# Hybrid encoder layer on one core: latent bias summed in part on VectorE, and three smaller edits in the front

## The chip, the cores and the metric

The kernel runs on one core of a Trainium2 chip. The metric is the device time in microseconds (us) of one execution; the time of a kernel is the median of several runs.

## The reference, cut to what matters

One encoder layer over 1024 tokens with 1024 features, batch 1, all in float32. It normalises and modulates the input, projects it, runs a pooling branch and a latent-attention branch, and projects back:

```python
c_act = silu(c)
shift, scale, gate = split(c_act @ ada_w + ada_b, 3)
xn   = rmsnorm(x, norm_g) * (1 + scale) + shift
proj = xn @ w_in
u_pool, g_pool, q_lat, kv_lat, k_rope_raw, g_attn = split(proj)   # 512, 512, 256, 128, 32, 512 columns
y_pool = multiscale_pool(u_pool, pool_w, pool_scale) * silu(g_pool)
q  = rmsnorm(q_lat, g_q_lat) @ w_uq           # 8 heads of 64 + 32 (rope)
kv = rmsnorm(kv_lat, g_kv_lat) @ w_ukv        # 8 heads of 64 (key) + 64 (value)
k  = concat(k_nope, k_rope_raw for every head)
q, k = rmsnorm(q, g_qnorm), rmsnorm(k, g_knorm)  # over the 96 features of a head, then rope
y_attn = softmax(q k^T / sqrt(96)) v * silu(g_attn)
out = x + gate * (concat(y_pool, y_attn) @ w_out)
```

Three things matter here. `shift` goes through the projection as a bias: (x*r*a + shift) @ W = r * ((x*a) @ W) + shift @ W, so every block of projected columns needs a bias row `shift @ W`. The columns q_lat, kv_lat and k_rope_raw (416 together) are called the latent block. The norm of a key takes in the squares of the 32 rope columns, which all heads share.

## The kernel before, in words

Features stand on the 128 partitions in eight blocks (index `k`), tokens in eight tiles of 128 (index `t`). Float32 products are made from two parts, a high part of reduced precision and the rest, as three matmuls (high by high, high by low, low by high). Five queues run beside each other: TensorE (T), VectorE (V), ScalarE (A), GpSimd (G) and SyncE (SY), which issues the loads. Each runs its instructions in order.

**Front** (lines 207 to 474, under `tc.manual_schedule()`: the order is the program's; instructions of later parts may be put between by the framework's planner).

1. `cb` is silu(c), laid over all partitions; it is made in two blocks of 512 columns, each by TensorE into a PSUM bank and by ScalarE from there (L218, L219).
2. For each `k`: `lat_load` loads a block of the scale weights (`asc`), of x and of the latent weights `wlr[k]`; `lat_scale` multiplies `asc` by `cb` and sums over the columns (`mod_col`, L108, a VectorE product with a running sum) into one column of `a_raw`, makes `a_col` from it, and ScalarE makes the high part of the scaled x (`xh[k]`); `lat_low` makes the rest. TensorE accumulates the latent block of seven token tiles (`lat_mm`, L234), and of the eighth behind the loop.
3. The shift: eight more `mod_col` (`shift_col`) fill `sh_raw`, and two additions (L382, L403) make `shift` for `k` 0 to 3 and 4 to 7.
4. `lat_bias(k)` (L397) multiplies `shift[:, k]`, laid over 128 columns, by `wlr[k]` and accumulates all eight `k` in the bank `pbl`. Each is two matmul instructions in the trace. The first four `k` run ahead of the end of feature tile 0, the other four behind it and behind the first two blocks of tile 1.
5. Behind them, in the same bank but at column 448, TensorE makes the bias of feature tile 0 (L409, eight `k`, one column each, 16 matmul instructions). ScalarE copies `pbl` to `lbias` (L428), VectorE copies column 448 into `bias_fm` (L464).
6. The up-projection's weights are scaled and split (`wuqh`, `wuql`, `wkvh`, `wkvl`: L424 to L430).
7. `lat_end(t)` (L449 to L452) scales the latent tile by the token's norm, adds `lbias`, and ScalarE sums the squares of its q and kv columns. `lat_rms` (from L459 on) makes the latent norms of four token tiles at a time. `v_range` (L437 to L443) takes the maximum over `pv`, a TensorE sum of squares of the value weights.

Feature tiles are the other twelve blocks of 128 projected columns. `fm_mm(i, ...)` (L170) runs the blocks `k0` to `k1` of tile `i`, six matmuls each, into two banks; `fm_weights` loads and splits a tile's weights; `fm_fold` (L152, L154) multiplies a tile's weights by `shift` on GpSimd and adds up the eight blocks in three halvings, and `fm_bias` sums the result over the partitions on TensorE. Tiles 2, 4, 6 and 8 to 11 are folded.

PSUM: the pool `psB` has seven banks (`bk`), the pool `psC` one (`sbk`, tag `sm`). `pst`, `pbl`, `pv`, the transposes `pt` of the next part and the small sums `psb` share that one bank, each waiting until the last reader of the one before it is done.

**Up-projection and pooling** (lines 477 to 715, ordered by the planner). Per token tile, `up_tr` transposes the latent tile (`pt`, L532; ScalarE copies it to `lth`, VectorE makes `ltl`), `up_tok` makes queries, keys and values (L548, L558) and their sums of squares `ssq`; its last two lines square the 32 rope columns of the tile on ScalarE, with a running sum into `kr2` (L568). `gains_of_qk`, called at the second token, ends with eight small GpSimd products (L513, L514). After the loop come `rope_key` and `up_norm`, which adds `kr2` to the key's sums and takes the reciprocal root. Then feature tiles 2 to 10 run with the pooling, and the attention and the output projection follow, in an order written by hand again.

Of the kernel before, what the change touches and what calls it, by code (L numbers as in the profile page):

```python
# [17 lines left out]
P = 128  # L18
# [40 lines left out]
def body(ctx, tc, small, cond, xT, ada_sc, ada_sh, ada_gt, w_lat, w_fm, pool_w, w_uq, w_ukv, gains, pos, w_out, out):  # L59
# [46 lines left out]
    def mod_col(dst, w, cb):  # L106

        V.scalar_tensor_tensor(w, w, 1.0, cb, ALU.mult, ALU.mult, accum_out=dst)  # L108
# [27 lines left out]
    def sbk(name):  # L136
        return smallp.tile([P, 512], F32, tag="sm", name=name)
# [11 lines left out]
        return raw, hi, lo  # L149

    def fm_fold(pb):
        G.tensor_tensor(pb, pb, shift.unsqueeze(2).broadcast_to([P, NK, P]), ALU.mult)  # L152
        for n in (4, 2, 1):
            G.tensor_tensor(pb[:, :n], pb[:, :n], pb[:, n:2 * n], ALU.add)  # L154

# [52 lines left out]
    with ExitStack() as pa:  # L208
# [41 lines left out]

        def lat_scale(k):

            mod_col(a_raw[:, k:k + 1], ascs[k], cb)
            V.tensor_scalar(a_col[:, k:k + 1], a_raw[:, k:k + 1], ab1[:, k:k + 1], ng_s[:, k:k + 1],
                            ALU.add, ALU.mult)
            A.activation(wlh[k], wlr[k], AF.Copy)
            V.tensor_tensor(wll[k], wlr[k], f32(wlh[k]), ALU.subtract)
            for c_ in (slice(0, 512), slice(512, S)) if k == 0 else (slice(0, S),):
                A.activation(xh[k][:, c_], xrs[k][:, c_], AF.Copy, scale=a_col[:, k:k + 1])
# [134 lines left out]
        pbl = sbk("pbl")  # L394

        def lat_bias(k):
            T.matmul(pbl[:, :LAT], shift[:, k:k + 1].broadcast_to([P, P]), wlr[k], start=k == 0, stop=k == NK - 1)  # L397

        for k in range(4):
            lat_bias(k)  # L400
# [2 lines left out]
        V.tensor_tensor(shift[:, 4:], sh_raw[:, 4:], adab_s[:, 4:8], ALU.add)  # L403
        fm_mm(0, fhi0, flo0, 6, 8)
        fm_mm(1, fhi1, flo1, 0, 2)
        for k in range(4, NK):
            lat_bias(k)
        for k in range(NK):
            T.matmul(pbl[:, 448:449], fraw0[:, k, :], shift[:, k:k + 1], start=k == 0, stop=k == NK - 1,  # L409
                     skip_group_check=True)  # L410


        wuqh = mp.tile([P, 2, 768], F32R, tag="wuqh", name="wuqh")
# [47 lines left out]

        for t in range(2):
            lat_end(t)
        V.tensor_copy(bias_fm[:, 0:1], pbl[:, 448:449])  # L464
        fm_mm(1, fhi1, flo1, 2, 5)
        pv = sbk("pv")
        T.matmul(pv, ones, sqv, start=True, stop=True)
        fm_mm(1, fhi1, flo1, 5, 6)
        for t in range(2, NK):
            lat_end(t)  # L470
            if t == 6:
                lat_rms(0, 4)
        v_range()
        lat_rms(4, NK)
# [15 lines left out]
    def gains_of_qk():  # L490


        gm = QT[:, NK - 1].rearrange("p h d -> p (h d)")[:, 0:192].rearrange("p (i c) -> p i c", i=3)
        for i, g_ in enumerate((ggk, gqr, gkr)):
            n = g_.shape[1]
            V.scalar_tensor_tensor(gm[:, i, :n], g_, -1.0, g_, ALU.mult, ALU.max)
            V.tensor_reduce(p2[:, i:i + 1], gm[:, i, :n], AX.X, ALU.max)
        V.tensor_scalar(p2[:, 0:3], p2[:, 0:3], 1e-15, 1e15, ALU.max, ALU.min)
        V.tensor_scalar(p2[:, 0:3].bitcast(I32), p2[:, 0:3].bitcast(I32), 0x7F800000, None, ALU.bitwise_and)
        V.tensor_tensor(p2[:, 3:4], p2[:, 1:2], p2[:, 2:3], ALU.mult)  # L500
        V.tensor_tensor(p2[:, 3:4], p2[:, 3:4], p2[:, 0:1], ALU.max)
        V.tensor_scalar(esc, p2[:, 3:4], 1.0 / 1024.0, None, ALU.mult)
        V.tensor_scalar(nesc, p2[:, 3:4], -1.0 / 1024.0, None, ALU.mult)
        V.reciprocal(ksc, p2[:, 3:4])
        V.tensor_scalar(ksc, ksc, 8.0, None, ALU.mult)
        V.tensor_scalar(gkr, gkr, p2[:, 1:2], None, ALU.mult)
        V.reciprocal(p2[:, 1:2], p2[:, 1:2])
        V.tensor_scalar(gqr, gqr, p2[:, 1:2], None, ALU.mult)
        cs, sn = KA[:, :, 0:16], KB[:, :, 0:16]
        for ta, tb_, g in ((TA, TB, gqr), (KA, KB, gkr)):  # L510
            for c_ in (slice(16, 32), slice(0, 16)):
                gb = g[:, c_].unsqueeze(1).broadcast_to([P, NK, 16])
                G.tensor_tensor(ta[:, :, c_], cs, gb, ALU.mult)  # L513
                G.tensor_tensor(tb_[:, :, c_], sn, gb, ALU.mult)  # L514

    V.tensor_tensor(ggk, gn[:, 0, 0:64], gn[:, 1, 0:64], ALU.mult)

    def rope_key():
# [21 lines left out]
    def up_tok(t, lth, ltl):  # L540
# [14 lines left out]
        for n in range(2):  # L555
            pk = bk(f"pk{t}{n}")
            for i, (l, r) in enumerate(((lth, wkvh), (lth, wkvl), (ltl, wkvh))):
# [6 lines left out]
        A.activation(VT[:, t, :, 0:64], pkv[1], AF.Copy, scale=rkv[:, t:t + 1])  # L564
        V.scalar_tensor_tensor(VT[:, t, :, 65:129], pkv[1], rkv[:, t:t + 1], VT[:, t, :, 0:64],
                               ALU.mult, ALU.subtract)
        jk = upl.tile([P, 32], F32, tag="jk", name=f"jk{t}", bufs=2)
        A.activation(jk, lat[:, t, 384:416], AF.Square, accum_out=kr2[:, t:t + 1])  # L568

    def up_norm():  # L570
        V.tensor_tensor(ssq[:, 1], ssq[:, 1], kr2.unsqueeze(2).broadcast_to([P, NK, H]), ALU.add)
        tmp = upl.tile([P, 2, P], F32, tag="lth", name="rh", bufs=2)
        rsqrt_(tmp, rqk.rearrange("p a t h -> p (a t h)"), ssq.rearrange("p a t h -> p (a t h)"), 2 * NK * H, 96)
        V.tensor_scalar(rqk[:, 0], rqk[:, 0], 128.0 * HD ** -0.5, None, ALU.mult)
        V.tensor_scalar(rqk[:, 1], rqk[:, 1], ksc, None, ALU.mult)
# [4 lines left out]
    for t in range(NK):  # L580
# [5 lines left out]
        up_tok(t, *lt)  # L586
        lt = nxt
    A.activation(yp[0], yp[0], AF.Silu, bias=bias_fm[:, 0:1])
    rope_key()
    up_norm()  # L590
    up.close()


# [600 lines left out]
```

## Time and profile before

| | |
|---|---|
| median of 3 runs | 501.46 us (501.36 to 502.86) |
| profiled execution, own time | 500.05 us |
| its span | 498.3 us |
| TensorE matmuls busy | 464.9 us (93%) |
| VectorE busy | 355.9 us (71%) |
| ScalarE busy | 253.8 us (51%) |
| GpSimd busy | 234.4 us (47%) |
| granted TensorE clock, mean | 0.996 |

The rows below count from the span's start. PE is TensorE's matmuls, PEld its weight loads, DVE is VectorE, ACT ScalarE, POOL GpSimd, SPq the queue that issues loads. L12 is line 12 of the kernel; where a helper records an operation the line is the helper's. A busy share over the whole span mixes stages with different limits, so stretches are read one by one.

### The profile page before, as it was taken

How to read it: one execution, taken by the hardware profiler on the slowest of the kernel's cores; microseconds unless marked ns; L12 is line 12 of the kernel's file. 1: busy time of each engine (PE TensorE's matmuls, PEld its weight loads, DVE VectorE, ACT ScalarE, POOL GpSimd, SP SyncE). 2: the span in 40 equal slices, each digit the busy share in tenths (PEclk: the TensorE clock that was granted, in tenths of full speed). 3: DMA queues.
4: the chain of work that ended last, by engine and by line, in shares of the span. 5: the costliest groups of instructions: out<-in, count | busy, mean ns of one | idle time of the engine just before them, and what ended most of it. 6: DMA issues, size and time to landing. Idle time of an engine off the chain costs nothing.

```text
span 498.3 us, 7657 instructions
## 1 busy us (share of the span) xinstructions
PE 464.9 (93%) x2956; PEld 355.0 (71%) x2956; DVE 355.9 (71%) x565; ACT 253.8 (51%) x338; POOL 234.4 (47%) x190
## 2 busy tenths in 40 slices
PE   5999998999999999999989888898898969999997
PEld 3999876898888888785555555555555658888886
DVE  4888849999999853577677887877867985913221
ACT  3756038993203030226878888888899861001000
POOL 1950040201242949448869796787869780000000
PEclk9999999999999999999999999999999999999999
DMA  8894442000102110144786779779982836753333
GB/s 300 332 307 159 171 142 65 6 1 7 47 1 91 34 58 27 57 86 95 170 148 138 162 145 176 152 151 163 224 175 63 160 113 231 276 182 129 126 128 126
DMA packets 117046, 66.33 MB, mean 133 GB/s; under 512 B 105873, under 2 KB 107793, under 8 KB 117010
## 3 DMA queue, kind: packets, MB, share of 16 engines
q1 hardware_dynamic: 117010, 65.85, 49.9%
q8 instruction: 23, 0.38, 0.3%
q14 instruction: 13, 0.11, 0.1%
HBM read 35.43 MB, written 4.19 MB: 80 GB/s over the span
## 4 chain that ended last, share of the span: by engine, by line
PE 49%; DVE 22%; ACT 10%; POOL 10%; issue 5%; DMA 3%; SPq 0%; ACTq 0%; DVEq 0%; POOLq 0%
PE ops L974 14%; PE fps L170 8%; PE st L800 4%; PE pq L548 3%; ACT ph L824 3%; PE lps L234 3%; DVE bp L808 3%; POOL fraw L152 3%; ACT p L819 3%; DMA wlr<-in_w_lat 2%; PE rs L730 2%; PE av L849 2%; PE st L804 2%; POOL s L614 2%; DVE ph L831 2%
## 5 line engine op out<-in xcount | busy, mean ns | idle before, releaser
L831 POOL TENSOR_TENSOR ph<-p,ph 128x1024 f16<-128x1024 f32 x49 | 105.9, 2168 | 13.1 <-ACT ph L824 10.2
L170 PE MATMUL fps<-xh,whi 128*128 128x512 f32 x192 | 62.0, 404 | 0.5 <-ACT whi L147 0.5
L170 PE MATMUL fps<-xh,wlo 128*128 128x512 f32 x192 | 59.3, 390 | 0.1
L170 PE MATMUL fps<-xl,whi 128*128 128x512 f32 x192 | 59.3, 390 | 0.0
L800 PE MATMUL st<-q,k 97*128 97x512 f16 x192 | 49.5, 379 | 6.7 <-ACT p L819 6.6
L804 PE MATMUL st<-k,q 97*128 97x512 f16 x192 | 48.2, 379 | 8.0 <-ACT p L819 6.4
L824 ACT ACTIVATE ph<-p 128x1024 f16<-128x1024 f32 x49 | 51.7, 1055 | 0.5
L152 POOL TENSOR_TENSOR fraw<-fraw,shift 128x1024 f32<-128x1024 f32 x7 | 22.7, 3237 | 60.8 <-DVE wlo L148 53.8
L808 DVE TENSOR_REDUCE bp<-st 128x1 f32<-128x1024 f32 x32 | 39.0, 1220 | 5.2 <-PE st L804 3.4
L170 PEld LDWEIGHTS fps<-xh,whi 128*128 128x128 f32 x192 | 35.5, 189 | 9.0 <-ACT whi L147 1.0
L170 PEld LDWEIGHTS fps<-xh,wlo 128*128 128x128 f32 x192 | 36.0, 188 | 8.1 <-DVE wlo L148 0.5
L170 PEld LDWEIGHTS fps<-xl,whi 128*128 128x128 f32 x192 | 36.1, 188 | 7.7
L935 ACT ACTIVATE owhi<-oraw 128x1024 fp32r<-128x1024 f32 (+1 forms) x10 | 8.8, 885 | 54.0 <-DMA oraw<-in_w_out 54.0
L819 ACT ACTIVATE p<-st,bp,esc 128x1024 f32<-128x1024 f32 x25 | 30.1, 1204 | 9.4 <-DVE bp L809 9.0
L804 PEld LDWEIGHTS <-q 97*128 97x128 f16 x192 | 16.6, 97 | 25.6 <-issue 10.9
L800 PEld LDWEIGHTS <-k 97*128 97x128 f16 x192 | 16.6, 97 | 21.5 <-issue 8.3
L624 ACT ACTIVATE dh<-s 128x1024 fp32r<-128x1024 f32 x4 | 4.2, 1062 | 51.9 <-DVE s L621 51.9
L819 ACT ACTIVATE p<-st,ebias,esc 128x1024 f32<-128x1024 f32 x24 | 28.9, 1203 | 2.5 <-PE st L800 1.3
L850 PE MATMUL av<-VT,ph 128*128 128x65 f16 x256 | 26.4, 193 | 2.9 <-POOL ph L831 2.9
L849 PE MATMUL av<-VT,pt 128*128 128x129 f16 x256 | 28.0, 221 | 0.8 <-DMA pt<-ph 0.8
L849 PE MATMUL av<-VT,ph 128*128 128x129 f16 x256 | 27.7, 221 | 0.2 <-DVE rb L869 0.2
L850 PEld LDWEIGHTS <-ph 128*128 128x128 f16 x256 | 22.6, 98 | 7.1 <-POOL ph L831 3.1
(297 smaller groups left out, 1142.5 us busy)
## 6 DMA issues: line engine op xcount, KB each, us to landing
fraw<-in_w_fm SPq DMA_DIRECT2D x12, 512.0 KB, 3.7
asc<-in_ada_sc SPq DMA_DIRECT2D x8, 512.0 KB, 6.0
xr<-in_xT SPq DMA_DIRECT2D x8, 512.0 KB, 5.3
ash<-in_ada_sh SPq DMA_DIRECT2D x8, 512.0 KB, 6.8
oraw<-in_w_out SPq DMA_DIRECT2D x8, 512.0 KB, 5.1
xres<-in_xT SPq DMA_DIRECT2D x8, 512.0 KB, 5.0
agt<-in_ada_gt SPq DMA_DIRECT2D x8, 512.0 KB, 5.7
out_dram<-xres SPq DMA_DIRECT2D x7, 512.0 KB, 3.0
```

Source lines behind the costliest of these rows:

```text
L152: G.tensor_tensor(pb, pb, shift.unsqueeze(2).broadcast_to([P, NK, P]), ALU.mult)
L170: T.matmul(ps[n], w[:, k, :], x_[k][:, n * 512:(n + 1) * 512], start=(k == order[0] and j == 0), stop=(k == order[-1] and j == 2))
L234: T.matmul(ps[:, :LAT], l[k][:, ts_], r[k], start=(k == 0 and i == 0), stop=(k == NK - 1 and i == 2))
L800: T.matmul(stt[i][:, n], l[:HW, kt * P:(kt + 1) * P], r[:HW, 0:512], start=(a == 0), stop=(a == 2))
L804: T.matmul(stt[i][:, n], l[:HW, qt * P:(qt + 1) * P], r[:HW, n * 512:(n + 1) * 512], start=(a == 0), stop=(a == 2))
L808: V.tensor_reduce(bps[i], stt[i], AX.XY, ALU.max)
L819: A.activation(pfs[i], st, AF.Exp, bias=bps.pop(i) if hf else ebias, scale=esc)
L824: A.activation(pas[i][:, 0], pfs[i], AF.Copy)
L831: (V if in_psum(i) else G).tensor_tensor(pas[i][:, 1], pfs[i], pas[i][:, 0], ALU.subtract)
L849: T.matmul(o_, hi, VT[:, kt, h, 0:129], start=kt == 0 and qt % 2 == 0, stop=False, skip_group_check=True)
L850: T.matmul(o_[:, 0:65], lo, VT[:, kt, h, 0:65], start=False, stop=kt == NK - 1, skip_group_check=True)
L974: T.matmul(ps[d][n], w_[:, k, :], y_[k][:, n * 512:(n + 1) * 512], start=(k == 0 and j == 0), stop=(k == NK - 1 and j == 2))
```

## The change

Four edits, all in the front or in the part behind it.

- The latent bias of `k` 4 to 7 is summed on VectorE into `lacc` (one scaling, three multiply-adds over 416 columns), and one matmul with a block of ones adds the partitions up into `pbl`. The bias column of feature tile 0 moves behind three blocks of tile 1, its copy into `bias_fm` behind the seventh `lat_end`, and `pv` gets a bank from the pool of seven.
- The first `mod_col` of the scale runs in two halves of 512 columns, into two columns of `sh_raw` that are added.
- The squares of the rope columns are made for all tokens at once: one GpSimd product into a part of `KT` that is not yet in use, and one VectorE reduction at the head of `up_norm`. `up_norm` now stands ahead of `rope_key`.
- The first product of a fold is queued on GpSimd behind the last gain product made so far (`tc.issue_after` fixes the order on the queue and adds no wait). For tile 2 that is the last product of `gains_of_qk`.

```diff
     def fm_fold(pb):
-        G.tensor_tensor(pb, pb, shift.unsqueeze(2).broadcast_to([P, NK, P]), ALU.mult)
+        with tc.issue_after(g_last[-1]):
+            G.tensor_tensor(pb, pb, shift.unsqueeze(2).broadcast_to([P, NK, P]), ALU.mult)
...
         def lat_scale(k):
 
-            mod_col(a_raw[:, k:k + 1], ascs[k], cb)
+            if k == 0:
+                for n in range(2):
+                    c_ = slice(n * 512, n * 512 + 512)
+                    mod_col(sh_raw[:, n:n + 1], ascs[0][:, c_], cb[:, c_])
+                V.tensor_tensor(a_raw[:, 0:1], sh_raw[:, 0:1], sh_raw[:, 1:2], ALU.add)
+            else:
+                mod_col(a_raw[:, k:k + 1], ascs[k], cb)
...
         def lat_bias(k):
-            T.matmul(pbl[:, :LAT], shift[:, k:k + 1].broadcast_to([P, P]), wlr[k], start=k == 0, stop=k == NK - 1)
+            T.matmul(pbl[:, :LAT], shift[:, k:k + 1].broadcast_to([P, P]), wlr[k], start=k == 0, stop=False)
...
         fm_mm(1, fhi1, flo1, 0, 2)
-        for k in range(4, NK):
-            lat_bias(k)
-        for k in range(NK):
-            T.matmul(pbl[:, 448:449], fraw0[:, k, :], shift[:, k:k + 1], start=k == 0, stop=k == NK - 1,
-                     skip_group_check=True)
+        lacc = ap.tile([P, LAT], F32, tag="lacc", name="lacc")
+        V.tensor_scalar(lacc, wlr[4], shift[:, 4:5], None, ALU.mult)
+        for k in range(5, NK):
+            V.scalar_tensor_tensor(lacc, wlr[k], shift[:, k:k + 1], lacc, ALU.mult, ALU.add)
+        T.matmul(pbl[:, :LAT], ones, lacc, start=False, stop=True)
...
         for t in range(2):
             lat_end(t)
-        V.tensor_copy(bias_fm[:, 0:1], pbl[:, 448:449])
         fm_mm(1, fhi1, flo1, 2, 5)
-        pv = sbk("pv")
+        for k in range(NK):
+            T.matmul(pbl[:, 448:449], fraw0[:, k, :], shift[:, k:k + 1], start=k == 0, stop=k == NK - 1,
+                     skip_group_check=True)
+        fm_mm(1, fhi1, flo1, 5, 6)
+        pv = bk("pv")
         T.matmul(pv, ones, sqv, start=True, stop=True)
-        fm_mm(1, fhi1, flo1, 5, 6)
         for t in range(2, NK):
             lat_end(t)
             if t == 6:
+                V.tensor_copy(bias_fm[:, 0:1], pbl[:, 448:449])
                 lat_rms(0, 4)
...
-                G.tensor_tensor(tb_[:, :, c_], sn, gb, ALU.mult)
+                g_last.append(G.tensor_tensor(tb_[:, :, c_], sn, gb, ALU.mult).ins)
+
+    g_last = []
...
-        jk = upl.tile([P, 32], F32, tag="jk", name=f"jk{t}", bufs=2)
-        A.activation(jk, lat[:, t, 384:416], AF.Square, accum_out=kr2[:, t:t + 1])
 
     def up_norm():
+        sq_ = KT[:, 6, :, 64:]
+        G.tensor_tensor(sq_, lat[:, :, 384:416], lat[:, :, 384:416], ALU.mult)
+        V.tensor_reduce(kr2, sq_, AX.X, ALU.add)
...
-    rope_key()
     up_norm()
+    rope_key()
```

## Rows read from the trace of the kernel before

**Rows 1.** Busy time by stretches: us, then PE, PEld, DVE, ACT, POOL.

```profile
83.50:115.35 31.85, 31.27 (x169) 27.84 (x169) 30.24 (x84) 29.92 (x73) 3.45 (x8) 1.00 0.06 17
115.35:209.50 94.15, 94.15 (x419) 77.44 (x417) 74.06 (x136) 16.76 (x18) 49.78 (x34) 1.00 0.12 38
209.50:212.00 2.50, 1.90 (x7) 1.15 (x7) 1.80 (x3) 0.67 (x1) 0.44 (x1) 1.00 0.44 177
```

**Rows 2.** Chain of waits, 68 to 101 us: start, us, what.

```profile
68.45 2.79 PE pbl L397 x8
71.24 1.68 PE pbl L409 x16
72.92 4.20 PE fps L170 x18
...
78.27 3.68 PE fps L170 x16
...
96.80 0.33 PE pt L532 x3
...
100.60 0.33 PE pt L532 x3
```

**Rows 3.** Waits of TensorE, 0 to 240 us: total, times, longest.

```profile
PE pt L532 <- DVE vmx L437: 1.0, 1, 1.0
PE pq L548 <- ACT lth L536: 0.6, 1, 0.6
```

**Rows 4.** Timeline of VectorE, 64 to 84 us: start, us, instruction, idle before.

```profile
64.85 0.16 DVE L403 TENSOR_TENSOR shift<-sh_raw,small 128x4 f32<-128x4 f32 x1
66.25 1.02 DVE L425 SCALAR_TENSOR_TENSOR wuql<-uqr,small,wuqh 128x768 fp32r<-128x768 f32 x1 [1.24 <-ACT wuqh L424]
67.20 1.22 DVE L148 TENSOR_TENSOR wlo<-fraw,whi 128x1024 fp32r<-128x1024 f32 x1
...
74.55 1.28 DVE L430 SCALAR_TENSOR_TENSOR wkvl<-ukr,small,wkvh 128x1024 fp32r<-128x1024 f32 x1 [5.19 <-ACT wkvh L429]
75.75 1.21 DVE L449 SCALAR_TENSOR_TENSOR lat<-lat,rstd,lbias 128x416 f32<-128x416 f32 x2
...
82.69 0.68 DVE L437 TENSOR_REDUCE vmx<-pv 128x1 f32<-128x512 f32 x1
```

**Rows 5.** Timeline of ScalarE, 64 to 83 us.

```profile
72.96 0.52 ACT L428 ACTIVATE lbias<-pbl 128x416 f32<-128x416 f32 x1 [4.97 <-PE pbl L409]
...
81.97 1.06 ACT L147 ACTIVATE whi<-fraw 128x1024 fp32r<-128x1024 f32 x1 [0.59 <-PE fps L170]
```

**Rows 6.** Groups of VectorE by form, 60 to 130 us: count, busy us, mean ns.

```profile
L553 DVE TENSOR_REDUCE ssq<-pq 128x4 f32<-128x384 f32 x16 | 8.6, 551 | 0.6 <-ACT pq L552 0.5
L449 DVE SCALAR_TENSOR_TENSOR lat<-lat,rstd,lbias 128x416 f32<-128x416 f32 x8 | 4.7, 645 | 0.0
...
L118 DVE TENSOR_SCALAR rh<-ssq 128x128 f32<-128x128 f32 x1 | 0.2, 221 | 0.0
```

**Rows 7.** Timeline, first microseconds; the last line is the first scale load's landing.

```profile
6.05 0.60 ACT L219 ACTIVATE cb<-pc 128x512 f32<-128x512 f32 x1 [1.11 <-PE pc L218]
...
6.68 1.23 DVE L108 SCALAR_TENSOR_TENSOR asc<-asc,cb 128x1024 f32<-128x1024 f32 x1 [3.49 <-ACT cb L219]
...
DMA to landing us min/median/max: 3.2/3.2/3.2
```

**Rows 8.** Groups of ScalarE by form, 83 to 86 us.

```profile
L568 ACT ACTIVATE jk<-lat 128x32 f32<-128x32 f32 x8 | 1.7, 219 | 0.0
```

**Rows 9.** Timeline of GpSimd, and the TensorE reader of the third tile's fold.

```profile
68.51 2.60 POOL L152 TENSOR_TENSOR fraw<-fraw,shift 128x1024 f32<-128x1024 f32 x1 [36.69 <-DVE wlo L148]
...
94.18 0.47 POOL L514 TENSOR_TENSOR KB<-KB,gn 128x128 f32<-128x128 f32 x1
...
126.28 0.28 PE L160 MATMUL psb<-ones,fraw 128*128 128x1 f32 x2
...
159.40 9.98 POOL L152 TENSOR_TENSOR fraw<-fraw,shift 128x1024 f32<-128x1024 f32 x1 [8.97 <-DVE wlo L148]
```

More of the change, by code (lines that the diff above doesn't have):

```diff
@@ L588, in body @@
     A.activation(yp[0], yp[0], AF.Silu, bias=bias_fm[:, 0:1])
+    up_norm()
     rope_key()
-    up_norm()
     up.close()
```

## The prediction

> **What bounds the kernel now.** I read the busy time by stretches first. TensorE works without a break from the first matmul of the third weight tile at 115.35 us to 209.5 us (94.15 of 94.15 us), loses about a microsecond there, and in the stretch before it, the per-token up-projection, it is busy for all but half a microsecond of 31.85 us [rows 1]. So what counts in the front is the time at which TensorE gets to its next piece of work; what other engines do there costs only where TensorE waits for it.
>
> The chain of waits says what that work is [rows 2]. From 68.45 us it is TensorE's own queue: the second half of the latent bias (2.79 us), the 16 one-column matmuls for the first tile's bias (1.68 us), then the second feature tile, up to 78.27 + 3.68 = 81.95 us. Then it leaves TensorE. The list of TensorE's waits [rows 3] shows the two that follow: the first transpose waits 1.0 us for VectorE's maximum over `pv` (L437), because `pt` and `pv` share the one-buffer bank, and the first up-projection matmul waits 0.6 us for ScalarE. The transposes start only when L437 ends, at 82.69 + 0.68 = 83.37 us [rows 4]. How much the up-projection itself stalls follows from its period: a token's transposes start at 96.80 us and the next token's at 100.60 us [rows 2], 3.80 us, so eight tokens are 30.4 us. From 81.95 us to 115.35 us [rows 1, 2] there are 33.4 us, hence 3.0 us of stalls: 1.45 us up to the first transpose, 1.55 us later.
>
> VectorE in the same place [rows 4] sat idle for 5.19 us before L430, since ScalarE could read the bias only at 72.96 us, after the last of the 16 matmuls that write the same bank [rows 5]. From 74.55 us on its queue is full.
>
> **Sum of the latent bias.** Eight matmul instructions (four column blocks, two each) take 2.79 us [rows 2]; one block stays, with `lacc` as moving operand: 2.79 / 4 = 0.70 us. TensorE loses 2.1 us of work. VectorE gains one scaling and three multiply-adds of 128x416. The multiply-add has the shape of L449, 0.645 us [rows 6]; the scaling is bounded by 0.22 us (L118, 128x128) and 0.645 us, and I take 0.45 us since it has the length of the one and the form of the other. That is 2.4 us (2.2 to 2.6) from 65.0 us, when the second half of `shift` is done [rows 4]: finished at 67.4 us. TensorE asks for it at 68.45 us [rows 2], so the wait that is added has 1 us to spare. Behind the four sums on VectorE stand `wuql` twice and the third tile's low part [rows 4]; these end about 2.4 us later, near 70.5 us, still before their readers, because of the 5.19 us idle stretch.
>
> **The first tile's bias column moves.** Its 1.68 us stay on TensorE, but behind 18 feature matmuls (4.20 us) and no longer ahead of the bias [rows 2]. ScalarE therefore reads the bias at 68.45 + 0.70 = 69.2 us and not at 72.96 us, and VectorE can begin the latent ends, which followed that read by 75.75 - 72.96 = 2.8 us [rows 4, 5], near 72.0 us: 3.8 us earlier. The copy into `bias_fm` is now behind the seventh latent end (72.0 + 7 x 0.6 = 76.2 us; two took 1.21 us, [rows 4]), and the column is done at 69.15 + 4.20 + 1.68 = 75.0 us, so it does not wait. On the SP queue, the load of the fourth tile's weights waits for this column to release its buffer and is issued 2 us later; its conversion waits for TensorE to end the second tile anyway [rows 5], so nothing waits for that.
>
> **`pv` gets a bank of its own.** `pt` now waits for the copy at 76.2 us and not for L437. TensorE reaches the end of the second tile at 81.95 - 2.1 = 79.9 us; the transpose is released before that. The 1.45 us up to the first transpose go. What is late next: ScalarE's copy of `pt`, VectorE's low part of it, and banks, since `pv` holds one of seven until L437 while the first two tiles hold four. I leave the other 1.55 us of stalls in place, because VectorE's queue moves forward by 3.8 us and TensorE by 3.5 us, so their distance stays. Ends: none of the 3.0 us goes, or all of it does. I take 1.4 us.
>
> **First scale column in halves.** ScalarE makes the first block of `cb` before the second, which ends at 6.05 + 0.60 = 6.65 us; the scale weights, issued as one of the first loads, land 3.2 us after their issue [rows 7]. So half of the 1.23 us product leaves the path [rows 7]. A line through 0.645 us (416 columns, [rows 6]) and 1.23 us (1024) gives 0.74 us for 512, that is 0.49 us less; the added one-column sum costs about 0.2 us (0.16 us for four columns, [rows 4], and its hand-over). Gain 0.3 us. With a half at 0.645 us it is 0.4 us, with a half as dear as the whole a loss of 0.2 us. The loads that follow are released by what starts here, so I let the 0.3 us through.
>
> **Rope key's squares.** Eight ScalarE squares of 0.22 us go [rows 8]; ScalarE is only the second wait of [rows 3], 0.6 us, and that is left in the sum. GpSimd gets a product of 128x256 on an idle queue (its neighbours: 0.47 us for 128x128, 2.60 us for 128x1024, [rows 9]), VectorE one reduction, between nothing and 0.55 us (L553, 128x384, [rows 6]). Hidden by VectorE's slack in the up-projection, otherwise 0.55 us ahead of `up_norm`; there TensorE has two feature tiles to work on [rows 1], so it shows only through the 1 us wait near 210 us. Putting `up_norm` ahead of `rope_key` pulls the same chain forward by about as much. Zero for both, 0.5 us either way.
>
> **Third tile's fold.** Its four GpSimd instructions move from 68.51 us behind the gain products, which end at 94.65 us. The reader is a TensorE matmul at 126.28 us [rows 9]: 26 us of cover; without it the fold's 2.6 us and what follows would count. Beside VectorE in the up-projection it should not hurt: the gain products there took their 0.47 us while VectorE read PSUM. Zero.
>
> **Sum.** 2.1 + 1.4 + 0.3 = 3.8 us. The profiled execution took 500.05 us (span 498.3 us); it lies 1.4 us under the median of 501.46 us, so 496.25 us for its like and 497.7 us for the median. Behind 115 us TensorE has no gap that could swallow it [rows 1], and the attention stage hangs on what ends here.
>
> **Rivals.** *Late sums.* The front's order is written by hand, but instructions from behind it are put between, as the third tile's `wlo` at 67.20 us [rows 4]. If it and `wuql` come before the sums, these start at 68.4 us and end at 70.8 us, and TensorE waits 2.4 us: 500.1 us. Against it: at 65.0 us neither has its input, since `wuql` waited 1.24 us for ScalarE.
>
> *The other chain holds.* TensorE's wait near 210 us ends a chain over VectorE, GpSimd and ScalarE. If that chain does not move with the up-projection, TensorE only waits longer there: 501.5 us. Against it: it starts from the last up-projection matmuls, which move.
>
> *A fold starved by VectorE.* This one ends slower. At 159.40 us one fold's first product took 9.98 us against 2.60 us [rows 9], next to VectorE's run of products out of SBUF. The section behind the front is ordered by a planner, and a shifted front may set a second fold beside such a run, on the chain that ends at 210 us. That adds 7.4 us: 501.5 - 3.8 + 7.4 = 505.1 us. It decides from 5.3 us of extra stall on. Against it: the relative times behind 115 us barely change. The Trainium skill, SBUF — State Buffer, section Who interferes with whom, says the shared port is locked for one instruction and the loser waits until that one has finished. By that rule a fold would lose one VectorE product, under a microsecond, and this rival would not end slower; the trace does not agree, since its fold lost over 7 us.
>
> **How the numbers follow.** A measurement of this kernel can tell about 0.3%, 1.5 us, from no change. My forecast has 0.72, with its own range of 496.1 us (all 3.0 us of stalls go) to 499.1 us (none). Late sums 0.09 and the other chain 0.09 lie within 1.5 us; the starved fold 0.10 is slower. Faster 0.72, same 0.18, slower 0.10. The range runs from 495.8 us (all stalls and the small gains) to 500.6 us, which takes in the late sums.
>
> **What would show it.** One block of bias matmuls and no wait before it; the bias read near 69 us; the first transpose released without L437 and the third tile's first matmul near 111.5 us, not 115.35 us; the same shift at 209 us. I am wrong if TensorE waits for `lacc`, if the 115.35 us point moves by under 2 us, or if it moves and the wait near 210 us grows.

## The result, and the profile after

The changed kernel is slower: 503.06 us (median of 7 runs) against 501.36 us of the kernel before beside it, ratio 1.0039, 95% interval 1.0024 to 1.0054. The forecast was 497.7 us. Its profiled execution took 503.25 us with a span of 501.4 us.

Busy time by stretches, as in [rows 1], with the third tile's first matmul now at 115.61 us:

```profile
83.50:115.61 32.11, 31.64 (x163) 28.28 (x162) 29.17 (x80) 27.75 (x54) 7.80 (x12) 0.95 0.05 17
115.61:173.00 57.39, 57.39 (x256) 47.38 (x255) 53.38 (x110) 9.93 (x11) 25.45 (x16) 1.00 0.10 32
173.00:212.00 39.00, 36.98 (x165) 29.98 (x163) 18.57 (x27) 7.24 (x7) 26.30 (x19) 1.00 0.16 51
```

The front ends where it ended (115.35 us before), at a mean granted clock of 0.95 and not 1.00. From 173 to 212 us TensorE is idle for 2.0 us, where the kernel before is idle for 0.6 us. Its list of waits, 40 to 245 us, lacks the first line of [rows 3]; the second has grown, and three waits are new (for `fraw`, `lacc` and `ltl`):

```profile
PE pq L559 <- ACT lth L547: 1.9, 1, 1.9
PE psb L161 <- POOL fraw L155: 1.5, 1, 1.5
PE pbl L417 <- DVE lacc L416: 0.8, 1, 0.8
PE fps L171 <- ACT whi L147: 0.6, 1, 0.6
PE pt L543 <- DVE ltl L548: 0.5, 1, 0.5
```

**The wait for `lacc`.** VectorE's timeline where [rows 4] had none of these sums:

```profile
64.45 0.44 DVE L414 TENSOR_SCALAR lacc<-wlr,shift 128x416 f32<-128x416 f32 x1
64.92 1.34 DVE L416 SCALAR_TENSOR_TENSOR lacc<-wlr,shift,lacc 128x416 f32<-128x416 f32 x2
66.83 1.23 DVE L148 TENSOR_TENSOR wlo<-fraw,whi 128x1024 fp32r<-128x1024 f32 x1 [0.57 <-ACT whi L147]
67.97 0.65 DVE L416 SCALAR_TENSOR_TENSOR lacc<-wlr,shift,lacc 128x416 f32<-128x416 f32 x1
```

The sums cost what was forecast (0.44 us, then 0.65 us each). But the planner put the third tile's low part between the third and the fourth, with 0.57 us of waiting for ScalarE ahead of it. So the fourth ends 1.7 us later, at 68.62 us.

**The wait for `lth`.** ScalarE's timeline, 80 to 83 us:

```profile
80.46 1.06 ACT L147 ACTIVATE whi<-fraw 128x1024 fp32r<-128x1024 f32 x1 [2.35 <-PE fps L171]
81.42 0.40 ACT L459 ACTIVATE ljk<-lat 128x256 f32<-128x256 f32 x1
...
82.24 0.49 ACT L547 ACTIVATE lth<-pt 128x384 fp32r<-128x384 f32 x1
```

The first transpose is out at 78.8 us, no longer held by `vmx`. Its copy, though, stands on ScalarE's queue behind the fourth tile's conversion, which waits for TensorE to end the second tile, and behind the last latent tile's squares. TensorE ends the tile at 80.87 us and stands idle up to 82.78 us:

```profile
80.26 0.61 PE L171 MATMUL fps<-xh,wlo 128*128 128x512 f32 x2
82.78 0.45 PE L559 MATMUL pq<-wuqh,lth 128*128 128x384 f32 x1 [1.91 <-ACT lth L547]
```

The kernel before had the same order on ScalarE. Behind the conversion at 81.97 us [rows 5] its queue ran without a gap up to the copy, so that the copy could hardly have come earlier, whatever released the transpose (ScalarE, then TensorE):

```profile
83.75 0.23 ACT L568 ACTIVATE jk<-lat 128x32 f32<-128x32 f32 x1
84.01 0.49 ACT L536 ACTIVATE lth<-pt 128x384 fp32r<-128x384 f32 x1
...
81.77 0.61 PE L170 MATMUL fps<-xh,wlo 128*128 128x512 f32 x2
84.55 0.45 PE L548 MATMUL pq<-wuqh,lth 128*128 128x384 f32 x1 [0.58 <-ACT lth L536]
```

From the end of the second tile to the first up-projection matmul it was 2.17 us (82.38 to 84.55 us, with the transposes in between), and now it is 1.91 us. The clock falls behind that wait; windows of 2 us from 82 us (the granted clock is the third number from the right; 0.50 is the 1.2 GHz level, called the half clock below):

```profile
82.00:84.00 2.00, 1.22 (x6) 1.18 (x7) 2.00 (x5) 0.70 (x3) 0.00 (x0) 0.96 0.19 25
84.00:86.00 2.00, 2.00 (x8) 1.56 (x7) 1.76 (x16) 1.19 (x2) 0.00 (x0) 0.50 0.64 238
86.00:88.00 2.00, 2.00 (x9) 2.00 (x9) 1.19 (x6) 1.21 (x3) 0.00 (x0) 0.69 0.00 0
```

**The wait for the fold.** VectorE at 142 us, then GpSimd (in the kernel before both halves of `u` stand together at 142.26 us, and the window sum starts at 143.69 us):

```profile
142.41 0.94 DVE L656 TENSOR_TENSOR QT<-QT,rqk 128x768 f32<-128x768 f32 x1
143.28 0.68 DVE L538 TENSOR_TENSOR u<-fps,rb 128x512 f32<-128x512 f32 x1
143.88 1.39 DVE L653 SCALAR_TENSOR_TENSOR yp<-pps,small,yp 128x512 f32<-128x512 f32 x2
145.19 0.67 DVE L538 TENSOR_TENSOR u<-fps,rb 128x512 f32<-128x512 f32 x1
...
146.19 1.21 DVE L148 TENSOR_TENSOR wlo<-fraw,whi 128x1024 fp32r<-128x1024 f32 x1
```

```profile
146.01 3.91 POOL L621 TENSOR_TENSOR s<-u 128x1038 f32<-128x1038 f32 x1 [6.69 <-DVE u L538]
...
161.02 10.32 POOL L153 TENSOR_TENSOR fraw<-fraw,shift 128x1024 f32<-128x1024 f32 x1 [7.30 <-DVE wlo L148]
171.42 3.55 POOL L155 TENSOR_TENSOR fraw<-fraw 128x512 f32<-128x512 f32 x3
```

A query product and two map products have come in between the halves of `u`. GpSimd's window sum starts late and lies beside VectorE's `wlo` and a key product, and its fold, the starved one of [rows 9] (159.40 us, 9.98 us), starts at 161.02 us and takes 10.32 us. The matmul `psb` waits 1.49 us for it.

**The scale in halves.** In the kernel before `a_col` follows ScalarE's second block of `cb` (6.65 us, [rows 7]) by 1.30 us; in the changed kernel, below it, by 0.96 us:

```profile
7.95 0.27 DVE L254 TENSOR_SCALAR a_col<-a_raw,ab,small 128x1 f32<-128x1 f32 x1
```

```profile
6.23 0.60 ACT L220 ACTIVATE cb<-pc 128x512 f32<-128x512 f32 x1 [1.11 <-PE pc L219]
...
6.86 0.69 DVE L108 SCALAR_TENSOR_TENSOR asc<-asc,cb 128x512 f32<-128x512 f32 x1 [1.01 <-ACT cb L220]
...
7.79 0.27 DVE L261 TENSOR_SCALAR a_col<-a_raw,ab,small 128x1 f32<-128x1 f32 x1
```

**One more, in the attention stage.** The chain of waits at 374 us:

```profile
374.87 5.42 DMA pt<-ph
380.33 0.23 PE av L861
```

This transpose of probabilities lands in 3.7 us in the first profile of the kernel before, where no matmul waits for it. Here TensorE waits 1.6 us for it.

**All profiles in one table.** Shift of TensorE against the first profile of the kernel before: start of the same matmul in the one less its start in the other (median of nine neighbours), in us, at seven times of the kernel before. What happens in a stretch is the difference of two columns.

| kernel | 66 | 129 | 180 | 230 | 356 | 382 | 484 |
|---|---|---|---|---|---|---|---|
| before, second profile | +0.87 | +0.87 | +0.92 | +0.86 | +0.88 | +1.21 | +1.91 |
| before, third | -0.30 | -0.30 | -0.29 | -0.28 | -0.30 | -0.06 | +0.70 |
| changed | -0.60 | +0.25 | +1.79 | +1.82 | +1.86 | +3.50 | +3.17 |
| changed, second | -0.82 | -1.34 | +0.20 | +0.26 | +0.34 | +1.74 | +2.62 |
| e1 sums first | +0.29 | +0.07 | +1.61 | +1.67 | +1.64 | +3.30 | +3.02 |
| e2 copy first | -0.13 | -1.34 | +0.20 | +0.84 | +0.59 | +2.32 | +2.05 |
| eF busy instead | -1.15 | -2.08 | -0.55 | +0.06 | -0.22 | -0.18 | -0.08 |
| eU window input first | -0.43 | -1.33 | +0.20 | -0.45 | -0.72 | +0.72 | +0.94 |
| uR rope key first | +0.79 | +1.35 | +1.34 | +1.87 | +1.61 | +3.03 | +3.24 |
| uB bias as before | -0.55 | +1.65 | +3.17 | +3.26 | +2.99 | +3.20 | +3.40 |
| e1R | -0.38 | -0.62 | -0.61 | -0.07 | -0.34 | +1.39 | +1.58 |
| e3R all three | -0.80 | -3.33 | -3.35 | -2.12 | -2.40 | -0.86 | -0.11 |
| e3R, second | +0.01 | -2.46 | -2.49 | -1.22 | -1.49 | +0.17 | +0.39 |
| e3R, third | -0.59 | -3.12 | -3.12 | -1.92 | -2.21 | -0.33 | -0.14 |
| aP changed, four more | -0.97 | -1.54 | -0.03 | -0.02 | -0.29 | -0.07 | +0.03 |
| e3P all three, four more | -0.38 | -2.89 | -2.94 | -1.68 | -1.97 | -2.05 | -1.88 |
| e3PB banks as before | -0.86 | -3.40 | -3.42 | -3.43 | -3.72 | -3.75 | -3.58 |

Up to 66 us executions of one code differ by over a microsecond, and behind 382 us again by up to 1.2 us (the changed kernel's two). Between, the two profiles of the changed kernel against the mean of three of the kernel before give: start -0.9, 66 to 129 us +0.2, 129 to 180 us +1.5, 180 to 356 us +0.1, 356 to 382 us +1.3, the rest -0.2; together about 2.0 us, where the medians differ by 1.7 us.

### The profile page after: what moved, and what is told of

Its sections match the earlier page's. It is cut to its first block, busy times and chain, and to the rows that moved or that the text cites. A ratio compares the mean times of both kernels' runs of the same rounds, so it can differ in the third digit from the quotient of the medians.

```text
span 501.4 us, 7638 instructions
## 1 busy us (share of the span) xinstructions
PE 463.8 (92%) x2950; PEld 354.3 (71%) x2950; DVE 357.5 (71%) x573; ACT 252.0 (50%) x322; POOL 236.4 (47%) x191
## 4 chain that ended last, share of the span: by engine, by line
PE 43%; DVE 24%; POOL 10%; ACT 10%; DMA 6%; issue 5%; SPq 0%; ACTq 0%; DVEq 0%; POOLq 0%
PE ops L986 14%; PE fps L171 6%; PE st L812 4%; DMA wlr<-in_w_lat 3%; PE pq L559 3%; ACT ph L836 3%; POOL fraw L153 3%; DVE bp L820 3%; ACT p L831 2%; POOL s L626 2%; PE av L861 2%; DMA pt<-ph 2%; PE st L816 2%; PE lps L235 2%; PE rs L742 2%
## 5 line engine op out<-in xcount | busy, mean ns | idle before, releaser
L861 PEld LDWEIGHTS <-pt 128*128 128x128 f16 x256 | 23.0, 97 | 8.4 <-DMA pt<-ph 3.6
```

Of the source, the lines that this page charges most:

```text
L861: T.matmul(o_, hi, VT[:, kt, h, 0:129], start=kt == 0 and qt % 2 == 0, stop=False, skip_group_check=True)
```

## Experiments

Each kernel is the changed one with one edit, or with several of them together. Ratios are against the kernel before on the same chip. Five places are taken up: the wait for `lacc` (e1), the copy of the first transpose (e2, eF), the fold (eU, uR, uB), the late transpose (aP, e3P) and a bank near 219 us (e3PB).

### The order in the front

**e1, sums first.** `s_last` collects the sums; `tc.issue_after` fixes an order on the queue.

```diff
-        V.tensor_tensor(lo, raw, f32(hi), ALU.subtract)
+        with tc.issue_after(s_last[-1]):
+            V.tensor_tensor(lo, raw, f32(hi), ALU.subtract)
```

> The changed kernel, but the third weight tile's low part on VectorE comes after the fourth bias sum and no longer before it. In the changed kernel's trace TensorE waits 0.8 us for `lacc`. My theory: this wait goes, but TensorE then only reaches the first up-projection matmul 0.8 us earlier and waits there for ScalarE's copy of the first transpose, 2.7 us and not 1.9 us; the third tile's first matmul stays within 0.3 us of 115.6 us and the time near 503.1 us. Rival: the wait for `lacc` is what was lost; the first up-projection matmul and all behind it come 0.8 us earlier, 502.3 us.

Ratio 1.0028 (1.0011 to 1.0045), 502.41 us. The wait for `lacc` is gone. My theory that it would be swallowed fell: the wait for `lth` stayed at 1.9 us, since it runs from TensorE's own end of the second tile (conversion, squares, copy). From 66 to 129 us e1 loses 1.07 us less than the changed kernel's first profile, both with the half clock. The first matmul of the third tile came only 0.17 us earlier, because this execution started 0.9 us later.

**e2, copy first.** `h_last[0]` is ScalarE's copy of the first transpose.

```diff
+        if i == 3:
+            with tc.issue_after(h_last[0]):
+                A.activation(hi, raw, AF.Copy)
+        else:
             A.activation(hi, raw, AF.Copy)
```

> The changed kernel, but on ScalarE the conversion of the fourth weight tile comes after the copy of the first token's transpose and no longer before it. My theory: TensorE's 1.9 us wait for that copy goes, and with it the stretch of half clock behind it (granted 0.50 from 84 to 87 us, worth about 1.65 us); the third tile's first matmul moves from 115.6 to about 112.1 us, the time to about 499.6 us. Rival one: the half clock has another cause and stays; only 1.9 us are gained, 113.7 and 501.2 us. Rival two: the stall comes back later in the up-projection, since VectorE and ScalarE are full there; 115.6 and 503.1 us.

Ratio 1.0018 (1.0000 to 1.0035), 502.07 us; third tile at 114.03 us. The wait for `lth` is gone and the clock is 1.00, so the mechanism holds, but only half of the expected 3.5 us came (1.6 us). The wait for `lacc` grew to 1.3 us, and in the up-projection TensorE waits 0.5 us for VectorE's `ssq`: rival two holds in part.

**eF, busy instead.** Eight more matmuls before the last block of the second tile.

```diff
-    fm_mm(1, fhi1, flo1, 6, 8)
+    fm_mm(1, fhi1, flo1, 6, 7)
+    for _ in range(4):
+        for n in range(2):
+            T.matmul(fm_ps[1][n], flo1[:, 6, :], xh[6][:, n * 512:(n + 1) * 512], start=False, stop=False)
+    fm_mm(1, fhi1, flo1, 7, 8)
```

> The changed kernel with eight more matmuls of 128x512 (one k block's low product taken five times in place of once, so that the second feature tile's values are not the reference's) at the end of the second feature tile, 8 x 0.23 = 1.85 us: TensorE is busy where it waited for ScalarE. My theory: the half clock behind the wait comes from TensorE standing idle, so the clock stays at 1.00 and the third tile's first matmul comes at about 114.0 us, time 501.4 us, although more work is done. Rival: the half clock has another cause; 115.6 and 503.1 us, or later if the wait stays too.

Ratio 1.0014 (0.9998 to 1.0031), 501.27 us; third tile at 113.28 us, clock 1.00. 1.85 us more of work did not make the kernel slower: from 66 to 129 us its profile is 0.4 us ahead of the changed kernel's second one, and the loss near 376 us is missing too (see *The late transpose*). It doesn't prove the cause of the half clock: the planner now also put the copy ahead of the conversion, as in e2.

**Is the half clock the kernel's?** Two more profiles of the kernel before and one of the changed kernel.

> The kernel before, unchanged, for a second profile. Five of the profiled kernels stood idle for 1.5 to 1.9 us near 82 us and then show a granted clock of 0.50 for 3 to 4 us; the kernel before (1.0 and 0.6 us of waits there) and one of the changed ones did not. Theory: whether the half clock follows that idle time differs from one execution to the next, and the first profile of the kernel before, 1.4 us under the median, is one that escaped; this one shows the half clock, with the third tile's first matmul near 117 us. Rival: in the kernel before the waits are too short and the clock stays at 1.00 each time; 115.4 us.

> The kernel before once more, for a third profile, with the same two theories. The second thing to see is the stretch near 376 us, where the changed kernels stand 1.4 to 1.8 us later against the first profile of the kernel before: if that shift is a matter of the execution, it is in the other profiles of the kernel before too; if the change makes it, it is in none.

> The changed kernel, unchanged, for a second profile. By the theory of chance the waits of 1.9 us near 82 us and of 1.5 us near 173 us come again to a tenth, because orders make them, while the half clock behind the first may be there or not; rival: the half clock is there again and belongs to the kernel.

These runs are single ones: 501.97 and 500.76 us for the kernel before, 502.68 us for the changed one. My theory fell for the kernel before: its clock was 1.00 in all three, with 1.0 or 1.1 and 0.6 us of waits. The changed kernel's second profile has the same waits of 1.9 and 1.5 us and full clock; the same windows as above:

```profile
82.00:84.00 2.00, 1.49 (x7) 1.38 (x8) 2.00 (x7) 0.60 (x2) 0.00 (x0) 1.00 0.26 66
84.00:86.00 2.00, 1.93 (x12) 1.54 (x11) 1.91 (x15) 1.74 (x3) 0.00 (x0) 1.00 0.53 197
```

From 66 to 129 us that is 1.37 us less than in the first profile (-0.52 against +0.85): the price of the half clock when it comes. Over all runs, of seven profiles with 1.9 us of idle time four show it (changed, e1, uR, e1R) and three don't (changed again, eU, aP); of four with 1.0 or 1.1 and 0.6 us one does (uB); of seven without such waits none. So here the half clock came only behind such waits, and not in each execution. What decides is not shown.

### The fold

**eU, window input first.** Both halves of `u` ahead of the map's products and of the third token's query work (cut: the program also makes `u` ahead of the map).

```diff
+            with tc.issue_after(u_last[-1]):
                 V.scalar_tensor_tensor(sg[:, c_], pp, ps_s[:, gi:gi + 1], sg[:, c_], ALU.mult, ALU.mult)
...
+            with tc.issue_after(u_last[-1]):
                 up_tail(2 * gi)
```

> The changed kernel, but near 143 us VectorE finishes the second window sum's input `u` before the third token's query work and before the map's two products, as in the kernel before. The front is not touched: third tile's first matmul at 115.6 us as in the changed kernel. My theory: GpSimd's window sum starts near 143.7 us and not 146.0 us, takes about 1.9 us and not 3.9 us, the first product of the fold starts near 159.5 us, and TensorE's wait near 211 us is 1.9 us shorter; time 501.2 us. Rival: the late start is not what delays the end; the wait stays and the time is 503.1 us.

Ratio 1.0021 (1.0006 to 1.0037), 502.44 us. The window sum takes 1.92 us, the wait for the fold is gone, and the fold isn't starved at all:

```profile
142.44 1.92 POOL L625 TENSOR_TENSOR s<-u 128x1038 f32<-128x1038 f32 x1 [4.71 <-DVE u L538]
...
158.33 2.62 POOL L153 TENSOR_TENSOR fraw<-fraw,shift 128x1024 f32<-128x1024 f32 x1 [9.18 <-DVE wlo L148]
```

But now the fifth tile's `wlo` is late, and TensorE waits 1.5 us for that near 151 us. One wait took the place of another, so the run couldn't say what had moved `u`. The first matmul of the third tile came at 114.03 us and not at the expected 115.6 us, at full clock.

**uR, rope key first.**

```diff
-    up_norm()
     rope_key()
+    up_norm()
```

> The changed kernel with one line taken back: `rope_key` stands ahead of `up_norm` again, as in the kernel before. My theory: this swap alone let the third token's query product and the map's two products in between the two halves of the second window sum's input `u`; with it undone GpSimd's window sum starts near 143.9 us and takes 1.9 us, and TensorE's wait of 1.5 us for GpSimd's fold near 173 us goes; the front is as in the changed kernel (third tile's first matmul 114.0 or 115.6 us, without or with the half clock), time 501.5 us. Rival: the wait near 173 us comes from the shifted front and stays; 503.1 us.

Ratio 1.0025 (1.0014 to 1.0036), 501.84 us. With this one line taken back the halves of `u` stand together again, and the wait for the fold is gone; from 129 to 180 us the shift is -0.01 us, against +1.51 to +1.54 us in all seven profiles that have the swap and not eU's order. GpSimd:

```profile
145.01 1.92 POOL L621 TENSOR_TENSOR s<-u 128x1038 f32<-128x1038 f32 x1 [4.50 <-DVE u L538]
...
160.72 9.99 POOL L153 TENSOR_TENSOR fraw<-fraw,shift 128x1024 f32<-128x1024 f32 x1 [8.97 <-DVE wlo L148]
```

So the swap is the cause, and the front isn't; the next run shows the same from the other side.

**uB, bias as before.** All of the latent bias and `pv` taken back (the diff of the change, reversed in `lat_bias`, `lacc`, the bias column and `pv`).

> The changed kernel with the latent bias as before: all eight blocks by TensorE, the first tile's bias column straight behind them, `pv` in the one-buffer bank. What is left of the change is the scale column in halves, the squares with the swap of `up_norm` and `rope_key`, and the later fold. Theory: the front is that of the kernel before less a small gain of the halves, third tile's first matmul 114.9 to 115.4 us at full clock, and the wait of 1.5 us near 173 us is there, because the swap makes it; time 502.5 us. Rival: the latent bias is what made the kernel slower, and without it the time is that of the kernel before or less, 501 us.

Ratio 1.0043 (1.0028 to 1.0058), 503.12 us: what is left of the change is slower by itself. The wait at the fold is there (1.4 us), without the change's front. The front was expected at full clock and was not; half clock from 85 us and 0.7 us of waiting for `ssq` put it 2.2 us back from 66 to 129 us.

### Together

**e1R** is e1 with uR's line; **e3R** adds e2's.

> The changed kernel with `rope_key` ahead of `up_norm` again, and with the third tile's low part behind the fourth bias sum. Theory: the waits of 0.8 us (for `lacc`) and 1.5 us (for the fold) go, both in full, since in the run with the sums first the wait for ScalarE's copy stayed at 1.9 us; 503.1 - 2.3 = 500.8 us. Rival: the 0.8 us is swallowed in the front and only the 1.5 us show; 501.6 us.

> As the run before it in this call, and ScalarE's copy of the first transpose comes ahead of the fourth tile's conversion too. All that TensorE waited for in the changed kernel and not in the kernel before is then gone. Theory: third tile's first matmul near 113.2 us, that is 0.8 us before that of the run with the copy first, and the shift of about 2 us against the kernel before holds to the end; time 499.2 us, faster than both kernels. Rival: VectorE sets the pace of the up-projection and gives the 0.8 us back; 114.0 and 500.0 us. Rival two: what is gained ahead of 115 us is lost behind it, at the fold near 173 us or near 221 us; 501.0 us.

e1R: 1.0016 (1.0001 to 1.0031), 501.78 us, with the half clock. e3R: 0.9978 (0.9967 to 0.9990), 499.92 us, faster than both kernels. Its third tile comes at 112.0 us, earlier than the 113.2 us expected. The first up-projection matmul follows the second tile at once (it ends at 79.61 us):

```profile
79.00 0.61 PE L176 MATMUL fps<-xh,wlo 128*128 128x512 f32 x2
79.67 0.44 PE L566 MATMUL pq<-wuqh,lth 128*128 128x384 f32 x1
```

From 66 to 129 us it gains 2.5 us and keeps it up to 216 us; then 1.2 us go in a wait for `gT` near 219 us and 1.5 us near 376 us. Two more profiles of e3R show the same two losses:

> The kernel with all three orders mended, for a second profile. Theory: no wait of over 1 us near 82 us, hence clock 1.00 up to 116 us, third tile's first matmul 112.0 us give or take the 0.8 us by which the start differs between executions, and a wait of about 1.2 us near 219 us for VectorE's `gT` that gives part of it back. Rival: the third tile's 112.0 us in the first profile was luck of the start; 113 us or later.

> The kernel with the three orders mended, again, as the measure for the two that follow. Expected 499.9 us, with waits of 1.2 us near 219 us (`gT`) and 1.4 us near 376 us (the transpose).

(The second, a single run of 500.44 us: third tile at 112.89 us, after a start that was 0.8 us later. The third: ratio 0.9982, 0.9969 to 0.9996, 499.88 us.)

### The late transpose

The stretch near 376 us costs 1.4 to 1.9 us in ten profiles of the table (all with the short bias sum but eF and the three at its end), and 0 to 0.3 us in three profiles of the kernel before and in uB. DMA traffic of the changed kernel, 374.5 to 381 us, in 40 slices:

```profile
GB/s 0 0 0 0 0 0 0 0 0 58 263 293 287 378 269 233 20 0 0 0 0 3 8 9 9 9 93 288 285 295 285 273 292 287 196 0 0 0 0 0
...
q8 instruction: 1, 0.02, 1.3%
issues: line engine op xcount, KB each, median us to landing
pt<-ph SPq DMA_TRANSPOSE x1, 5.4
```

One packet of instructions (1.3% of 16 x 6.5 us is 1.35 us of one DMA engine) falls into the transpose; for five slices (0.8 us) only some 9 GB/s move, and the rest of this transpose and the next one come behind that. Less the shift at 356 us, the packet's quarter of a microsecond begins between 374.25 and 375.00 us (eight times of ten at 374.75) in the profiles that lose there, and at 373.00 or 373.25 us in the three profiles of the kernel before, in eF and in uB. Over all 18 profiles the transpose takes 5.2 to 5.7 us to land in the first group and 3.7 to 4.0 us in the others. The first group differs from the others in TensorE's instruction count: three bias matmuls fewer (2950 matmul instructions in the profile, against 2956 in the kernel before and in uB, and 2958 in eF). **aP** and **e3P** put four tiny ones, eight instructions, where TensorE waits anyway (2.7 to 3.0 us, near 6 us):

```diff
             A.activation(cb[:, n * 512:(n + 1) * 512], pc, AF.Silu)
+        for _ in range(4):
+            T.matmul(pc[:, 0:1], ones[0:1, :], crow[:, 0:1], start=True, stop=True)
```

> The changed kernel with four more matmuls of one column on TensorE right behind the condition's two, at 6 us, where it waits 2.7 us for ScalarE anyway (their result is overwritten bank space that nobody reads). Theory: the load of TensorE's instructions comes about as many instructions earlier in the attention stage, ahead of the transpose and not inside it; the transpose near 376 us lands in 3.7 to 4.0 us, TensorE's wait of 1.4 to 1.6 us for it goes, and the time falls from 503.0 to 501.5 us. Rival: the late transpose has nothing to do with the instruction load; the wait stays and the time too, 503.0 us.

> The kernel with the three orders mended and the four more matmuls of one column at 6 us. Theory: the wait of 1.4 us near 376 us goes as in the first run of this call; 498.5 us. Rival: it stays; 499.9 us.

aP: 1.0012 (0.9995 to 1.0030), 500.88 us, 0.2 us waited at that place. The packet comes at 373.00 us, ahead of most of the transpose's traffic, and the transpose lands in 4.0 us (372.4 to 378.9 us, 40 slices):

```profile
GB/s 0 0 101 0 0 0 0 0 0 134 279 271 135 9 27 276 287 293 288 291 288 295 285 69 0 0 117 288 285 115 2 0 0 0 0 0 0 0 0 0
...
q8 instruction: 1, 0.02, 1.2%
issues: line engine op xcount, KB each, median us to landing
pt<-ph SPq DMA_TRANSPOSE x1, 4.0
```

e3P: 0.9961 (0.9946 to 0.9976), 498.46 us, 1.4 us under e3R beside it. Four matmuls whose result nobody reads are worth what was expected, in two pairs of kernels: the position of the instruction load was the cause.

### The banks

**e3PB** gives each of six such matmuls a bank of its own; with `pv` that makes seven, a full turn.

```diff
+        for j in range(6):
+            T.matmul(bk(f"pad{j}")[:, 0:1], ones[0:1, :], crow[:, 0:1], start=True, stop=True)
```

> As the run before it, but six matmuls of one column, each into a PSUM bank of its own, so that with the bank of `pv` seven more are taken from the rotation of seven and every later tile has the bank that it had in the kernel before. Theory: the wait of 1.2 us near 219 us is for a bank that the rotation handed out too early; it goes, and the one near 376 us too; 497.3 us. Rival: it comes from VectorE's order and stays; 498.5 us.

0.9922 (0.9902 to 0.9942), 496.54 us (4 runs): 4.3 us under the kernel before and 1.9 us under e3P. No wait for `gT` is left; TensorE's whole list, 40 to 245 us:

```profile
PE pq L568 <- DVE ssq L573: 0.8, 1, 0.8
PE fps L176 <- ACT whi L151: 0.6, 1, 0.6
```

So the wait near 219 us goes when the banks stand in their old turn (the two more matmuls can have a part in the 1.9 us). The rival, VectorE's order, is out: from 206.8 to 219.5 us VectorE has the same instructions in the same order in e3R and e3PB. That the changed kernel, e1 and aP, with the turn that `pv` shifted, show no wait there, and e2, eF, eU, uR and e1R a shorter one of 0.5 us, for `bias_fm`, the runs don't explain.

## Why the prediction was wrong

The sign was wrong. The term that failed most in the front is the 1.4 us for `pv`'s bank; what was lost behind the front stood in the sum at nothing. The parts, in the order of the prediction:

- **Stalls.** The 3.0 us between 81.95 and 115.35 us aren't in the rows: TensorE is idle there for 1.0 + 0.6 us [rows 3], and the rest is work, since the first tokens take longer than the 3.80 us of the one that was read. The sum took 1.4 us of the 3.0 us; the lower end of the range took all.
- **Sum of the latent bias.** The work was right: one block is left, and the next matmul starts 0.5 us behind it, where the four blocks took 2.79 us; the sums took 0.44 and 0.65 us. "1 us to spare" was wrong. The rival *Late sums* had the mechanism (the planner puts `wlo` in), with one instruction ahead of the last sum in place of two ahead of all four: 0.8 us, not 2.4 us. Its argument against, that the input would not be ready, was no protection: the order was fixed beforehand, and VectorE stood idle for 0.57 us until that input came.
- **Bias column.** ScalarE read the bias at 69.68 us (forecast 69.2 us).
- **`pv` in its own bank.** The transpose was released without `vmx`, as forecast. The step that failed: "its conversion waits for TensorE to end the second tile anyway, so nothing waits for that". I asked who waits for the conversion's result and not what stands behind it on ScalarE's queue; there stood the first transpose's copy. The 1.4 us of this term measured 0.26 us (2.17 us from the end of the second tile to the first up-projection matmul, then 1.91 us), because ScalarE's queue had stood just behind `vmx` as the next bound. With the copy ahead of the conversion (e3R) it is 0.06 us. In four of seven profiles with that wait the half clock came on top; it cost 1.4 us where one kernel was profiled with it and without it.
- **Scale in halves.** The size was right where the edit acts. From the end of ScalarE's second block of `cb` to `a_col` it is 1.30 us in all three profiles of the kernel before and 0.96 us in all 15 of the changed ones. The first latent matmul gains the same 0.34 us in ten of these 15; in the other five ScalarE's `wlh`, which stands ahead of `xh` on its queue, ends after `a_col`. Up to 66 us the changed kernels lie 0.6 us under the kernel before in the means, but executions differ by 1.9 us.
- **Squares and the swap.** "Zero for both" was the second step that failed: the swap of the two calls costs 1.5 us (the squares' own cost was not separated). I priced it by what it delays and not as a new input to the planner, which ordered VectorE's queue anew some 30 us later.
- **Fold.** Zero was right: no wait at its reader near 126 us. The wait near 210 us, 0.6 us by [rows 1] and not 1 us, stayed as it was, so the rival *The other chain holds* did not come.
- **"Behind 115 us TensorE has no gap that could swallow it".** Wrong in three places: the fold at 173 us (1.5 us), a bank at 219 us (1.2 us in e3R), the transpose at 376 us (1.4 to 1.9 us). The rival *A fold starved by VectorE* named the place and the engine of the first; the fold starved already came later, no second one was added, and 1.5 us decided where 5.3 us were thought to be needed, since the front's gain was not there.

With these out of the way the kernel is 4.3 us under the kernel before, for a forecast of 3.8 us, but that this comes so near is partly luck. From 66 to 129 us it is 2.5 us in each of e3R, e3P and e3PB, not the forecast 3.5 us; in e3PB's one profile about 1 us comes from the start, and the rest from stretches for which nothing was forecast. In e3R the first up-projection matmul comes 4.1 us earlier (79.67 us for 84.55 us, less the 0.8 us of the start), more than forecast, but the up-projection then takes 32.4 us in place of 30.8 us. The prediction had left its stalls as they were. 0.8 us of it stands in the list as a wait for `ssq`, the last reader of a bank. `pv`'s bank doesn't make that wait, since uB has it too (0.7 us); which edit does, the runs don't say.

## What to carry to other kernels

When a wait is removed ahead of an in-order queue, look at each instruction that stands between the newly released one and its result on the next engine; a conversion for a later tile that waits for the very same engine turns into the new bound. Where a planner orders the part behind, every edit, even a swap of two calls, is an edit to all queues behind it: compare the orders, and fix those on which a chain without slack depends. Before a part is given up as useless, follow its gain stretch by stretch; here it went in five separate places, and each could be mended by an order, a bank or four idle matmuls.

## What the runs showed of the hardware

- A load of instructions during the execution (0.02 MB, 1.35 us on one DMA engine) delays a DMA transpose that it meets: 5.2 to 5.7 us to landing in the ten profiles where it begins inside the transpose, 3.7 to 4.0 us in the other eight. Four more matmuls on TensorE 370 us earlier moved it out of the way.
- After the same 1.9 us of idle time the granted clock fell to 0.50, the 1.2 GHz level, in four profiles and stayed at 1.00 in three. It cost 1.4 us in the changed kernel, which was profiled with it and without it.
- GpSimd beside VectorE's products out of SBUF: the window sum took 3.91 us with `wlo` and a key product beside it and 1.92 us without, the fold's first product 9.98 to 10.32 us beside the run of query and key products and 2.62 us in eU, where VectorE fell idle 0.9 us after it began. VectorE loses too where GpSimd comes first: in uR `wlo`, begun 0.2 us behind a step of the window sum, took 2.93 us and not 1.21 us. The Trainium skill, SBUF — State Buffer, section Who interferes with whom, says that a VectorE product with two SBUF inputs contends with a GpSimd instruction that reads SBUF. On that the trace agrees; that the loser waits for one instruction only, as the prediction drew from that section, it contradicts with over 7 us.
